# A hybrid transformer on one core: the first layer's heads in pairs, in a TensorE order written out by hand

## The chip, the cores and the metric

The kernel runs on one core of a Trainium2 chip. The metric is the device time of one execution in microseconds. It has one launch, and every input is read from HBM. In the text PE is TensorE (matmuls, transposes), DVE is VectorE, ACT is ScalarE, POOL is GpSimd and SP is SyncE, which issues most of the loads.

## What is computed

Two blocks in a row for 512 tokens of width 1024, all in fp32. The first block has a gated delta layer and a layer of stick-breaking attention; the second has sliding-window attention beside an mLSTM, and a PEER feed-forward. The change touches the gated delta layer alone. Cut to what matters:

```python
mod = silu(c) @ w_ada[layer] + b_ada[layer]          # "conditioning": shift, scale, gate
h = rms(x, norm_g) * (1 + scale) + shift
proj = h @ w_in                                      # 4096 columns: q, k, v, z of 8 heads of 128, and b, a
qkv = silu(causal_conv(proj[..., :3 * W], conv_w))   # 4 taps
q, k = l2norm(q) * Dh ** -0.5, l2norm(k)             # per head
# chunks of 64 tokens; g is the cumulated log-decay of a chunk
L = strict_lower((k_beta @ k.T) * decay)
u, w = solve(L + I, [v_beta, k_beta * exp(g)])       # triangular, 64 x 64
attn = lower((q @ k.T) * decay)
def step(S, ...):                                    # 8 chunks, one after the other
    v_new = u_i - w_i @ S
    o = q_dec_i @ S + attn_i @ v_new
    S = S * g_last_i + k_dec_i.T @ v_new
o = rms(o, o_gain) * silu(z)
x = x + gate * (o @ w_out)
```

The second layer of the block, its keys and values (`w_kv`) and the whole second block follow. Their conditioning (24 + 16 rows of 128 outputs) depends on `c` alone and is computed during the first layer.

## The kernel before

**Projections.** Activations lie transposed, width on the partitions. An fp32 product is made of three matmuls in a split format: each operand has a high and a low part (`hH`, `hL` for the activations, `wh`, `wl` for the weights), and `mm3` multiplies high by high (L106), high by low (L107) and low by high (L108). `wtile` loads a block of 128 weight columns and makes the parts two k-slices at a time: ACT the high one (L99), POOL the low one (L102), or DVE, where the running number of the weight tile (`uid`) divides by 9. One block of 128 output columns is 8 x 3 matmuls over 512 tokens. Column block `cb` is q of head `cb` for 0 to 7, k for 8 to 15, v for 16 to 23, z for 24 to 31. The result goes through `conv` (ACT, then DVE with L444 among others, tile `y`) or `silu_z`.

**One head** (`gdn_head`, L526 to L671). *Preparation*: norms of q and k from column sums, the transposes of k and v (L542 and on), decay matrices `A` and `B`, the products k·k and q·k (L576), the transposes of `B` (L589, L595), short DVE instructions on 4 columns (L546, L561) and short powers on POOL (`cols`, L549). *Inverse*: the 64 x 64 triangular matrices of all 8 chunks, two to a 128 x 128 tile, are inverted by doubling in 5 levels (L605 to L625). A level is: the masked block `Lm` on POOL (L607), the transposes of X (L611, from the second level on), 4 matmuls Y = Lm X (L616), a copy by ACT (L618), 4 matmuls (L621), and the new X by DVE (L623). Then the inverse is multiplied with `vb` and `kw` (L628 to L632). *Recurrence*: 8 chunks, each with `s<-S,WQ` (L646), u on DVE, `s<-kd,u` (L650) and the new S on DVE (L655). *Tail*: attn times u, the output's norm, transposes, and `oT`.

**Order before.** `project(0)`, then for each head `gdn_head` and the next head's `project`, in plain program order. A scheduler with a model of the engines' times then moves each engine's instructions; so projection matmuls of later heads already stand between the levels of an inverse, and heads overlap, as far as tiles have buffers and PSUM has tags (`n` with two buffers, one each of `v0`, `v1`, `s0`, `s1`, two `pj`). No line fixes PE's order.

**Conditioning.** `ada` loads 128 rows of weights (512 KB) into one of two buffers. The 48 late rows (gate of this layer, all of the next) are started by `aside`, one after each new X and each `oT`. Two are DVE reductions; 46 are a product on POOL (L176, tile `ada`), a sum on ACT (L177) and an addition on DVE (L178).

**Start and end of the layer.** Under the first norm, while the conditioning of this layer comes in, the column blocks `FIRST` = 0, 8, 16 are projected k-slice by k-slice as the norm delivers them; `A0` and `WB` are buffer counts there. At the end `residual` projects with `w_out` in two parts of k: heads 0 to 6 for all 8 blocks, then head 7 (`EARLY_A`); partial sums are added to x, the squares of the new x are added up, and PE's column sums (L114) open the next norm.

Of the kernel before, what the change touches and what calls it, by code (L numbers as in the profile page):

```python
# [10 lines left out]
F32 = mybir.dt.float32  # L11
# [8 lines left out]
P = 128  # L20
# [13 lines left out]
class Net:  # L34
# [187 lines left out]

    def wtile(self, w, j0, n=2, ks=slice(0, KC)):
# [25 lines left out]
    def proj_T(self, w, j0, nblk, act, cb, ks=slice(0, KC)):  # L249

        H, L = act
        for g in range(0, nblk, self.blocks):
# [5 lines left out]
            for j in range(n):  # L258
                p = self.pj()
                for k in range(ks.start, ks.stop):  # L260
                    wh, wl = at(k)
                    self.mm3(p, wh[:, j], wl[:, j], H[:, k], L[:, k], k == ks.start, k == ks.stop - 1)
                cb(g + j, p)
# [25 lines left out]
    def residual(self, w, act, gate, x_in, x_out, scratch=None, parts=(slice(0, KC),)):  # L289

        nc = self.nc
# [12 lines left out]
        for ks in parts:  # L304
            self.proj_T(w, 0, KC, act, lambda j, p: cb(j, p, ks is parts[0], ks is parts[-1]), ks=ks)
# [21 lines left out]
class Gdn(Net):  # L327
    SPARE_SB, SPARE_2, SPARE_P = "pj pj l l", "pj pj l l", "pj pj s s"
    RAW, SB_, PART = 3, 3, 2
    FIRST, OFF, A0, WB, SPARE_0, SQ = (0, 8, 16), (), 12, 6, "v0", 8  # L330
    SP = 5
    YB = 8
    EARLY_A, EARLY_OUT = (slice(0, 7), slice(7, 8)), (slice(0, 6), slice(6, 8))
    RATE, LV = 1.0, 100
    S1, S2, S3, R1 = (3, 4), (6, 2), (3, 4), 3

    def gdn(self):
# [5 lines left out]
        with ExitStack() as st:  # L343
            self.ring(1, self.RAW, self.SB_, self.PART)
            self.psum(st, n=2, v0=1, v1=1, s0=1, s1=1)
# [10 lines left out]
            with tc.tile_pool(name="g_t", bufs=2) as tmp, tc.tile_pool(name="g_ada0", bufs=self.A0) as ap0:  # L356
                xT = self.xtile("x0")
                self.ada_setup(ac, ap)
                for k in range(KC):
# [3 lines left out]
                    self.FIRST, (self.pj(), self.pj(), self.pg("s0"), self.pg("v0"), self.pg("v1")))}  # L363
                w16 = [tmp.tile([P, KC, 40], dt, name=f"w16{n}", bufs=1) for n, dt in (("", F32), ("h", F32R), ("l", F32R))]
                r = self.rstd(tmp, xT, "l0", psum="n")
                pba = self.pg("s1")
# [22 lines left out]
            self.spare = self.SPARE_0.split()  # L389
# [89 lines left out]
            def project(h):  # L479
                for cb in range(h, 32, 8):  # L480
                    done = (lambda j, p: conv(cb, p)) if cb < 24 else lambda j, p: silu_z(h, p)
                    if cb in first:
                        done(0, first[cb])
                    else:
                        self.proj_T(w, cb, 1, act, done)
# [5 lines left out]
            self.dump("oT", oT)  # L491
            while late or came:
                if came:
                    came.pop(0)()
                if late:
                    came.append(self.ada(ap, *late.pop(0), len(late) % self.LV != 0))
            oH = hp.tile([P, KC, T], F32R, tag="hH", name="oH")
            oL = hp.tile([P, KC, T], F32R, tag="hL", name="oL")
            for k in range(KC):
                self.split(oH[:, k], oL[:, k], oT[:, k])  # L500
            x1 = {}
# [6 lines left out]

            class Out:
# [5 lines left out]
            self.residual(a["w_out_a"], (oH, oL), self.mod0[:, 16:24], x_in, Out(), parts=self.EARLY_A)  # L515
# [10 lines left out]
    def gdn_head(self, hd, h, q, k, v, z, gcol, rows, oT):  # L526
# [3 lines left out]
        self.tag = "n"  # L530
        new = lambda tag, shape, bufs=1: hd.tile([P] + shape, F32, tag=tag, name=f"{tag}{h}", bufs=bufs)
        late = lambda tag, shape, bufs=1: self.hs.tile([P] + shape, F32, tag=tag, name=f"{tag}{h}", bufs=bufs)
        v4 = lambda t: t.rearrange("p (i c) -> p i c", i=NT)
# [16 lines left out]
        kw, kd, vb = new("kw", [NT, P], 2), late("kd", [NT, P], 2), new("vb", [NT, P], 2)  # L550
# [3 lines left out]
        kb = new("kb", [T])  # L554
        nc.vector.tensor_tensor(kb, k, self.rows_of(bk), op=ALU.mult)
        sq = new("sq", [T], 2)
        nc.scalar.activation(sq, q, AF.Square)
        p = self.pg()
        self.colsum(p, sq, 1)
        r = self.rsqrt(hd, p[:, :NT], [NT], 1.0, f"q{h}", bufs=2)  # L560
        nc.vector.tensor_scalar(rq, r, DH_SCALE, None, op0=ALU.mult)  # L561
        pG = self.rep(h, rows)
        eg = new("eg", [T])
        nc.scalar.activation(eg, pG, AF.Exp)
        A, B = late("A", [NT, P], 3), new("B", [NT, P], 2)
# [4 lines left out]
        nc.gpsimd.tensor_tensor(B, A, strm.unsqueeze(1).to_broadcast([P, NT, P]), op=ALU.mult)  # L570
        for i2 in range(0, NT, 2):
# [7 lines left out]

        WQ = late("WQ", [NT, 2, 2, 64], 2)  # L580
        c4 = lambda ap: ap.rearrange("p (i b c) -> p i b c", i=NT, b=2)
        for b in range(2):
            nc.gpsimd.tensor_tensor(WQ[:, :, b, 1 - b], c4(q)[:, :, b], c4(eg)[:, :, b], op=ALU.mult)
        gl = late("gl", [8], 2)
        nc.gpsimd.tensor_copy(gl, eg.rearrange("p (n c) -> p n c", c=64)[:, :, 63])

        p = self.pg()
        for i in range(NT):
            nc.tensor.transpose(p[:, i * P:(i + 1) * P], v[:, i * P:(i + 1) * P], self.ident)  # L589
        nc.vector.tensor_tensor(rk, rk, gcol[:, 1, :, h], op=ALU.mult)  # L590
        nc.vector.tensor_tensor(vb, v4(p), rk.unsqueeze(2).to_broadcast([P, NT, P]), op=ALU.mult)
# [6 lines left out]
        self.tag = v = f"v{h % 2}"  # L598
# [1041 lines left out]
```

## Time and profile before

| | |
|---|---|
| median of 3 runs | 2853.34 us (2845.3 to 2853.7) |
| the profiled execution | 2852.8 us, of which the trace spans 2851.0 us |
| PE busy | 2671.3 us (94%), 14601 instructions |
| DVE busy | 1786.9 us (63%) |
| ACT busy | 1210.9 us (42%) |
| POOL busy | 1765.5 us (62%) |

A matmul is pipelined and its end is modelled, so a busy PE is not PE at its peak. Busy shares are means over stages: the first layer takes the first 520 us or so of the span, and POOL is busier there than in the middle of the kernel. In rows of groups the columns are: line, engine, operation, output and inputs, shape, count | busy us, mean ns of one | idle time of the engine before them, and what ended it.

### The profile page before, as it was taken

To read this page: it belongs to the slowest core of one execution; us is meant where nothing else is said; L and a number is where in the kernel's file an instruction comes from. 1 tells how busy PE (TensorE), PEld (TensorE's weight loads), DVE (VectorE), ACT (ScalarE), POOL (GpSimd) and SP (SyncE) were. 2 spreads that over 40 slices of the span, in tenths; PEclk is the share of its full clock that TensorE was granted. 3 is DMA by queue.
4 is the path that set the end of the run, shared out by engine and by line. 5 is a ranking of instruction groups with operands and counts; after the bars stand their busy time and mean duration, and the time that the engine had idled before them with its cause. 6 is when DMAs were issued, how large, how long until landed. Compare 5 with 4: busy or idle time off the path is not lost. (4 is left out here: it accounts for less than half of the span.)

```text
span 2851.0 us, 40457 instructions
## 1 busy us (share of the span) xinstructions
PE 2671.3 (94%) x14601; PEld 2266.0 (79%) x14601; DVE 1786.9 (63%) x3095; ACT 1210.9 (42%) x2508; POOL 1765.5 (62%) x1335
## 2 busy tenths in 40 slices
PE   6999898799998999999998989998998999999999
PEld 4877777697776877778786988898998978877777
DVE  7767664614446654122332989899899166778886
ACT  5566663636654454233333333333333333333332
POOL 4889883533333522433463468788788378888786
PEclk9999999899998999999999999999999999999999
DMA  6334331221011111221222587887987879999996
GB/s 240 108 119 125 111 113 31 76 90 60 31 39 54 56 45 60 74 69 66 69 79 89 160 296 261 284 290 256 314 277 281 276 272 344 340 333 331 333 328 227
DMA packets 206793, 499.35 MB, mean 175 GB/s; under 512 B 18304, under 2 KB 106624, under 8 KB 203520
## 3 DMA queue, kind: packets, MB, share of 16 engines
q1 hardware_dynamic: 167856, 359.19, 37.6%
q0 software_dynamic: 36864, 134.23, 13.1%
q10 hardware_dynamic: 1872, 3.33, 0.4%
q8 instruction: 115, 1.88, 0.3%
q14 instruction: 86, 0.70, 0.1%
HBM read 444.26 MB, written 52.43 MB: 174 GB/s over the span
## 5 line engine op out<-in xcount | busy, mean ns | idle before, releaser
L102 POOL TENSOR_TENSOR wl<-wr,wh 128x256 fp32r<-128x256 f32 (+2 forms) x499 | 414.8, 850 | 499.2 <-ACT wh L99 468.5
L102 POOL TENSOR_TENSOR upl<-upr,uph 128x1024 fp32r<-128x1024 f32 x128 | 312.9, 2445 | 97.0 <-ACT uph L99 96.3
L99 ACT ACTIVATE wh<-wr 128x256 fp32r<-128x256 f32 (+2 forms) x556 | 228.7, 445 | 302.6 <-PE pj L107 120.4
L106 PE MATMUL pj<-nH,downh 128*128 128x384 f32 x1024 | 354.3, 346 | 2.3 <-ACT w L1459 1.7
L108 PE MATMUL pj<-nH,downl 128*128 128x384 f32 x1024 | 349.6, 341 | 4.6 <-DVE downl L102 4.6
L107 PE MATMUL pj<-nL,downh 128*128 128x384 f32 x1024 | 348.8, 341 | 0.0
L102 POOL TENSOR_TENSOR downl<-downr,downh 128x1024 fp32r<-128x1024 f32 x96 | 243.9, 2542 | 129.3 <-ACT downh L99 126.4
L1504 PE MATMUL acc<-uph,wwh 128*128 128x512 f32 x768 | 302.7, 399 | 6.9 <-ACT wwh L99 6.9
L1504 PE MATMUL acc<-upl,wwh 128*128 128x512 f32 x768 | 305.4, 398 | 0.0
L99 ACT ACTIVATE downh<-downr 128x1024 fp32r<-128x1024 f32 x128 | 135.4, 1059 | 307.0 <-PE pj L107 163.2
L102 DVE TENSOR_TENSOR wwl<-wo,wwh 128x384 fp32r<-128x384 f32 x128 | 196.1, 1533 | 76.4 <-ACT wwh L99 70.5
L1504 PE MATMUL acc<-uph,wwl 128*128 128x512 f32 x768 | 232.4, 398 | 6.6 <-DVE wwl L102 6.5
L108 PE MATMUL pj<-hH,wl 128*128 128x512 f32 x544 | 222.8, 411 | 0.9 <-POOL wl L102 0.8
L106 PE MATMUL pj<-hH,wh 128*128 128x512 f32 x544 | 220.5, 405 | 2.1 <-ACT mo L1175 1.1
L107 PE MATMUL pj<-hL,wh 128*128 128x512 f32 x544 | 215.8, 397 | 0.0
L99 ACT ACTIVATE uph<-upr 128x1024 fp32r<-128x1024 f32 x128 | 134.8, 1053 | 174.9 <-POOL upl L102 116.1
L106 PEld LDWEIGHTS pj<-nH,downh 128*128 128x128 f32 x1024 | 193.7, 189 | 6.6 <-ACT w L1459 2.0
L108 PEld LDWEIGHTS pj<-nH,downl 128*128 128x128 f32 x1024 | 193.3, 189 | 5.3 <-DVE downl L102 4.9
L107 PEld LDWEIGHTS pj<-nL,downh 128*128 128x128 f32 x1024 | 193.6, 189 | 0.0
L1428 POOL DMA_INDIRECT gdown<-in_peer_down,idx x128 | 165.7, 1295 | 44.3 <-issue 13.7
L1504 PEld LDWEIGHTS acc<-uph,wwh 128*128 128x128 f32 x768 | 145.6, 190 | 44.6 <-ACT wwh L99 9.4
L1504 PEld LDWEIGHTS acc<-uph,wwl 128*128 128x128 f32 x768 | 144.8, 189 | 43.4 <-DVE wwl L102 8.3
(621 smaller groups left out, 6702.2 us busy)
## 6 DMA issues: line engine op xcount, KB each, us to landing
downr<-in_peer_down_j SPq DMA_DIRECT2D x128, 512.0 KB, 4.8
upr<-in_peer_up_j SPq DMA_DIRECT2D x128, 512.0 KB, 6.3
wr<-in_w_in SPq DMA_DIRECT2D x50, 512.0 KB, 4.2
ada<-in_w_ada SPq DMA_DIRECT2D x48, 512.0 KB, 3.7
wait<-w SPq DMA_DIRECT2D x128, 192.0 KB, 4.9
wo<-wait SPq DMA_DIRECT2D x128, 192.0 KB, 5.2
G<-stage SPq DMA_DIRECT2D x24, 1024.0 KB, 6.9
Gt<-G SPq DMA_DIRECT2D x48, 512.0 KB, 8.0
```

The lines of the kernel that those rows point to most:

```text
L99: nc.scalar.activation(h, src, AF.Copy)
L102: return (eb or nc.vector).tensor_tensor(l, src, h.bitcast(F32), op=ALU.subtract)
L106: mm(out, lh, rh, start=start, stop=False)
L107: mm(out, lh, rl, start=False, stop=False)
L108: mm(out, ll, rh, start=False, stop=stop)
L1428: nc.gpsimd.indirect_dma_start(out=g, out_offset=None, in_=self.a[f"peer_{name}"], in_offset=bass.IndirectOffsetOnAxis(ap=self.idx[:, s:s ...
L1504: mm(po[z][b], lh[:, zs], rh[:, bs], start=False, stop=j == P - 1 and rh is uh and lh is l, skip_group_check=True)
```

## The change

The first layer is written in another order, and PE's order in it is fixed.

- `in_order` wraps the heads and the output projection: each PE instruction that is written inside must stand behind the one written before it. Only PE is ordered so; the other engines remain the scheduler's.
- `gdn_head` is cut into `gdn_prep`, `gdn_inverse`, `gdn_recur` and `gdn_tail`, generators that yield between steps; `proj_steps` and `residual_steps` yield after each k-slice (three matmuls). `weave` runs several generators in turn and gives `n` steps of a filler for each of their steps.
- Heads go in pairs. The inverses of two heads run in step, with the tails of the pair before and six projection blocks (k, q, v of the next two heads; 2 slices for a step). Then the two recurrences run in step, filled with the preparations of the next pair and their z projections (1 step for a step). The last pair is filled with the output projection (0.8 after 12 steps, then 0.5).
- `FIRST` is 0, 8, 16, 1, 9: five column blocks under the norm. `A0` 12 → 10, `WB` 6 → 10. PSUM has six buffers of one tag `n` and two of `pj`.
- `kw` is made by one DVE instruction for each head in place of four on ACT; the matmuls with `kw` come ahead of those with `vb`; the order inside the preparation is another. `kd`, `A`, `WQ` and `gl` have four buffers, `eg` and `kb` two. `EARLY_A` is heads 0 to 5, then 6 and 7.

Weight tiles get other running numbers, so other ones fall to DVE: 111 low parts in place of 57 in the whole kernel, nearly all of the difference behind this layer.

```diff
+    def in_order(self):
+        tc, bb = self.tc, self.nc.cur_bb.bb
+        n = len(bb.instructions)
+        yield
+        last = None
+        for i in list(bb.instructions)[n:]:
+            if i.engine == mybir.EngineType.PE:
+                if last is not None:
+                    tc.add_manual_dep(i, last.name, mybir.DependencyInfo(
+                        mybir.DependencyClass.NoSync, mybir.DependencyReason.DATA), reason="in_order")
+                last = i
...
-    FIRST, OFF, A0, WB, SPARE_0, SQ = (0, 8, 16), (), 12, 6, "v0", 8
+    FIRST, OFF, A0, WB = (0, 8, 16, 1, 9), (), 10, 10
-    EARLY_A, EARLY_OUT = (slice(0, 7), slice(7, 8)), (slice(0, 6), slice(6, 8))
-    RATE, LV = 1.0, 100
+    EARLY_A, EARLY_OUT = (slice(0, 6), slice(6, 8)), (slice(0, 6), slice(6, 8))
+    RATE = 1.0
+    FILL, PREP = 2.0, 1.0
...
-            self.psum(st, n=2, v0=1, v1=1, s0=1, s1=1)
+            self.psum(st, n=6)
...
-            project(0)
-            for h in range(H_):
-                self.gdn_head(hd, h, y.pop(h), y.pop(8 + h), y.pop(16 + h), y.pop(24 + h), gcol, rr, oT)
-                if h + 1 < H_:
-                    project(h + 1)
...
+            def weave(main, fill, n, skip=0):
+                main, owed, at = list(main), 0.0, 0
+                while main:
+                    for g in list(main):
+                        if next(g, self) is self:
+                            main.remove(g)
+                            continue
+                        at += 1
+                        if at > skip:
+                            owed += n
+                            run(fill, int(owed))
+                            owed -= int(owed)
...
+            with self.in_order():
+                run(project(0, 8, 16, 1, 9))
+                f = project(17, 24)
+                weave([prep(0)], f, 2)
+                run(f)
+                f = project(25)
+                weave([prep(1)], f, 1)
+                run(f)
+                tails = []
+                for h in range(0, H_, 2):
+                    last = h + 2 == H_
+                    if last:
+                        split_o(*range(h - 2))
+                        fill = self.residual_steps(a["w_out_a"], (o_["H"], o_["L"]), self.mod0[:, 16:24],
+                                                   x_in, Out(), parts=self.EARLY_A)
+                    else:
+                        fill = project(8 + h + 2, h + 2, 16 + h + 2, 8 + h + 3, h + 3, 16 + h + 3)
+                    weave([*tails, *(self.gdn_inverse(hd, h + e, heads[h + e]) for e in range(2))],
+                          fill, *((0.8, 12) if last else (self.FILL, 0)))
+                    rec = [self.gdn_recur(h + e, heads[h + e]) for e in range(2)]
+                    tails = [tail(h + e) for e in range(2)]
+                    if last:
+                        weave(rec, fill, 0.5)
...
+                    else:
+                        run(fill)
+                        fill = both(prep(h + 2), prep(h + 3), project(24 + h + 2, 24 + h + 3))
+                        weave(rec, fill, self.PREP)
+                        run(fill)
+                        for g in tails:
+                            run(g, 1)
...
-        for o, c in ((kw, kwc), (kd, gcol[:, 3, :, h])):
-            for i in range(NT):
-                nc.scalar.activation(o[:, i], pk[:, i * P:(i + 1) * P], AF.Copy, scale=c[:, i:i + 1])
+        nc.vector.tensor_tensor(kw, v4(pk), kwc.unsqueeze(2).to_broadcast([P, NT, P]), op=ALU.mult)
+        for i in range(NT):
+            nc.scalar.activation(kd[:, i], pk[:, i * P:(i + 1) * P], AF.Copy, scale=gcol[:, 3, i, h:h + 1])
```

On PE, inside an inverse, the scheduler's order before (the level's matmuls are L616 and L621, the projection's L106 to L108; numbers behind a name tell tiles apart):

```order
L616 MATMUL v049_744<-Xv00_730,Lmv00_735 128x128 x4
L108 MATMUL pj143_1935<-hH_106,wl143_1947 128x512
L106 MATMUL pj143_1935<-hH_106,wh143_1946 128x512
L107 MATMUL pj143_1935<-hL_107,wh143_1946 128x512
L108 MATMUL pj143_1935<-hH_106,wl143_1947 128x512
L106 MATMUL pj143_1935<-hH_106,wh143_1956 128x512
L107 MATMUL pj143_1935<-hL_107,wh143_1956 128x512
L616 MATMUL v180_1202<-Xv11_1194,Lmv11_1200 128x128 x4
```

And PE inside the first inverse of the changed kernel (there the transposes of X are L729, Y is L734):

```order
L729 MATMUL n81_1288<-c_id_74,Xv00_1239 128x128 x4
L734 MATMUL n82_1295<-Xv00_1239,Lmv00_1286 128x128 x4
L106 MATMUL pj84_1304<-hH_106,wh84_1305 128x512
L107 MATMUL pj84_1304<-hL_107,wh84_1305 128x512
L108 MATMUL pj84_1304<-hH_106,wl84_1306 128x512
L106 MATMUL pj84_1304<-hH_106,wh84_1305 128x512
L107 MATMUL pj84_1304<-hL_107,wh84_1305 128x512
L108 MATMUL pj84_1304<-hH_106,wl84_1306 128x512
L729 MATMUL n85_1317<-c_id_74,Xv11_1261 128x128 x4
L734 MATMUL n86_1324<-Xv11_1261,Lmv11_1315 128x128 x4
```

Before, a head's level was followed by what the scheduler found ready; now two slices of projection (six matmuls) stand between a half level of one head and that of the other, always.

On POOL, before, between the inverses (`ada` is a conditioning product, `wl` a weight split):

```order
L176 TENSOR_TENSOR ada90_1275<-ada90_1275,c_rep_118 128x1024
L102 TENSOR_TENSOR wl149_2100<-wr148_0_2086,wh149_2099 128x256
L607 TENSOR_TENSOR Lmv11_1305<-Ls1_1192,c_lv5_455 128x512
L102 TENSOR_TENSOR wl149_2110<-wr148_0_2086,wh149_2109 128x256
L176 TENSOR_TENSOR ada94_1303<-ada94_1303,c_rep_118 128x1024
L602 TENSOR_TENSOR XTv02_1709<-Ls2_1706,c_lv0_445 128x512
L607 TENSOR_TENSOR Lmv02_1714<-Ls2_1706,c_lv1_447 128x512
L102 TENSOR_TENSOR wl149_2120<-wr148_0_2086,wh149_2119 128x256
L176 TENSOR_TENSOR ada98_1331<-ada98_1331,c_rep_118 128x1024
```

And POOL in the changed kernel ahead of and in the preparation of heads 2 and 3 (beside the first recurrence):

```order
L176 TENSOR_TENSOR ada136_2083<-ada136_2083,c_rep_118 128x1024
L102 TENSOR_TENSOR wl112_1650<-wr111_0_1646,wh112_1649 128x256
L102 TENSOR_TENSOR wl116_1726<-wr111_0_1646,wh116_1725 128x256
L176 TENSOR_TENSOR ada138_2105<-ada138_2105,c_rep_118 128x1024
L102 TENSOR_TENSOR wl122_1800<-wr111_0_1646,wh122_1799 128x256
L176 TENSOR_TENSOR ada139_2133<-ada139_2133,c_rep_118 128x1024
L651 TENSOR_TENSOR cols2_1587<-kss2_1588,mhalf_72 128x4
L651 TENSOR_TENSOR cols3_1617<-kss3_1618,mhalf_72 128x4
L176 TENSOR_TENSOR ada140_2143<-ada140_2143,c_rep_118 128x1024
L176 TENSOR_TENSOR ada148_2210<-ada148_2210,c_rep_118 128x1024
```

Before, one product stands for every two to four other instructions; now they stand closer together, also between the short powers of a preparation. In the changed kernel the 46 products are spread as follows: 10 in the stretch of the first inverse and its preparation, 33 from the first recurrence to the end of the second, 3 in the third inverse, none behind it.

## Rows read from the trace of the kernel before

**Rows 1.** PE's timeline: start us, us, engine, line, form, count [wait and releaser].
```profile
524.32 1.87 PE L114 MATMUL pj<-c_one,xi 128*128 128x1 f32 x8 [5.26 <-DVE xi L198]
```
**Rows 2.** Windows: stretch, us, busy (instructions) PE, PEld, DVE, ACT, POOL, clock, DMA, GB/s.
```profile
0.00:76.00 76.00, 48.97 (x193) 34.74 (x194) 58.72 (x86) 38.92 (x72) 39.04 (x40) 1.00 0.64 231
117.00:440.00 323.00, 296.58 (x1824) 252.59 (x1822) 220.54 (x391) 199.07 (x514) 279.24 (x234) 0.97 0.35 115
...
sum 40.00, PE 36.95 PEld 30.64 DVE 32.88 ACT 27.14 POOL 39.60; mean PE 18.48 PEld 15.32 DVE 16.44 ACT 13.57 POOL 19.80
```
**Rows 3.** PE's timeline in a preparation and inverse; then one group of instructions.
```profile
166.09 0.39 PE L107 MATMUL pj<-hL,wh 128*128 128x512 f32 x1
166.32 0.38 PE L576 MATMUL n<-kb,y 128*128 128x128 f32 x2
166.54 0.39 PE L576 MATMUL n<-y,y 128*128 128x128 f32 x2
...
171.31 0.60 PE L589 MATMUL n<-c_id,y 128*128 128x128 f32 x4
171.74 1.06 PE L632 MATMUL v<-Xv,kw 128*128 128x128 f32 x8
...
L616 PE MATMUL v<-Xv,Lmv 128*128 128x128 f32 x320 | 45.3, 288 | 3.4 <-ACT XTv L613 2.7 <-POOL Lmv L607 0.6
```
**Rows 4.** PE's waits from 0 to 525 us: total us, count, longest.
```profile
PE v L611 <- DVE Xv L623: 7.9, 5, 5.6
```
**Rows 5.** POOL's groups from 60 to 525 us.
```profile
L102 POOL TENSOR_TENSOR wl<-wr,wh 128x256 fp32r<-128x256 f32 (+2 forms) x143 | 114.0, 805 | 65.9 <-ACT wh L99 61.7 <-PE pj L107 3.1 <-PE s L650 0.6
L176 POOL TENSOR_TENSOR ada<-ada,c_rep 128x1024 f32<-128x1024 f32 x46 | 110.7, 2407 | 5.6 <-DMA ada<-in_w_ada 2.9 <-DMA ada<-in_w_ada_kv 2.0 <-PE pj L108 0.3
L607 POOL TENSOR_TENSOR Lmv<-Ls,c_lv 128x512 f32<-128x512 f32 x40 | 51.5, 1288 | 13.5 <-PE v L616 13.5
L583 POOL TENSOR_TENSOR WQ<-y,eg 128x256 f32<-128x256 f32 x16 | 11.4, 734 | 1.0 <-PE s L646 0.9
L570 POOL TENSOR_TENSOR B<-A,c_str 128x512 f32<-128x512 f32 x8 | 11.3, 1409 | 0.5 <-ACT A L569 0.4
L549 POOL TENSOR_TENSOR cols<-kss,mhalf 128x4 f32<-128x4 f32 x8 | 9.4, 1169 | 1.4 <-DVE cols L548 1.1 <-ACT th L446 0.3
```
**Rows 6.** A group on DVE from 60 to 525 us.
```profile
L444 DVE SCALAR_TENSOR_TENSOR y<-pj,cwh,y 128x509 f32<-128x509 f32 (+2 forms) x69 | 50.8, 743 | 19.4 <-ACT y L442 18.5
```
**Rows 7.** PE's timeline, from the preparation of head 0 to its first level.
```profile
75.67 0.44 PE L542 MATMUL n<-c_id,y 128*128 128x128 f32 x2
...
95.22 0.60 PE L595 MATMUL n<-c_id,B 128*128 128x128 f32 x4
...
100.24 0.83 PE L616 MATMUL v<-Xv,Lmv 128*128 128x128 f32 x6
```
**Rows 8.** Groups of ACT and DVE in a level, from 60 to 525 us.
```profile
L618 ACT COPY Yv<-v 128x512 f32<-128x512 f32 x40 | 23.6, 590 | 23.4 <-PE v L616 23.0
L623 DVE TENSOR_TENSOR Xv<-Xv,v 128x512 f32<-128x512 f32 x40 | 27.3, 682 | 20.4 <-PE v L621 20.2
```
**Rows 9.** PE's timeline in the recurrence of head 7: two chunks in a row.
```profile
449.94 0.49 PE L646 MATMUL s<-S,WQ 128*128 128x128 f32 x2 [0.44 <-DVE S L655]
...
452.60 0.39 PE L646 MATMUL s<-S,WQ 128*128 128x128 f32 x2
```
**Rows 10.** Window of 100 us behind the layer, in the columns of rows 2.
```profile
1200.00:1300.00 100.00, 98.55 (x587) 79.06 (x585) 19.52 (x50) 32.58 (x96) 39.77 (x56) 1.00 0.21 69
```
**Rows 11.** Timelines of DVE, POOL and PE around 146 us.
```profile
146.28 9.93 DVE L561 TENSOR_SCALAR cols<-rv_q 128x4 f32<-128x4 f32 x1
...
135.78 2.36 POOL L176 TENSOR_TENSOR ada<-ada,c_rep 128x1024 f32<-128x1024 f32 x1
...
155.44 0.75 POOL L102 TENSOR_TENSOR wl<-wr,wh 128x256 fp32r<-128x256 f32 x1
...
157.46 1.97 PE L611 MATMUL v<-c_id,Xv 128*128 128x128 f32 x8 [5.56 <-DVE Xv L623]
```

More of the change, by code (lines that the diff above doesn't have):

```diff
@@ L1 @@
 import math
-from contextlib import ExitStack
+from contextlib import ExitStack, contextmanager
 import numpy as np
@@ L477, in gdn, with project @@
             self.aside = aside
-            def project(h):
-                for cb in range(h, 32, 8):
-                    done = (lambda j, p: conv(cb, p)) if cb < 24 else lambda j, p: silu_z(h, p)
+            def project(*cbs):
+                for cb in cbs:
+                    done = (lambda j, p, cb=cb: conv(cb, p)) if cb < 24 else lambda j, p, cb=cb: silu_z(cb - 24, p)
                     if cb in first:
@@ L484, in project @@
                     else:
-                        self.proj_T(w, cb, 1, act, done)
-            project(0)
-            for h in range(H_):
-                self.gdn_head(hd, h, y.pop(h), y.pop(8 + h), y.pop(16 + h), y.pop(24 + h), gcol, rr, oT)
-                if h + 1 < H_:
-                    project(h + 1)
[L491 to L501, printed above, removed]
+                        yield from self.proj_steps(w, cb, 1, act, done)
             def x_in(j):
@@ L507, in x_in @@
                 return t
+            x1, heads, o_ = {}, {}, {}
             class Out:
@@ L514, in __getitem__, with prep, split_o @@
                     return x1[0][at]
-            self.residual(a["w_out_a"], (oH, oL), self.mod0[:, 16:24], x_in, Out(), parts=self.EARLY_A)
+            def prep(h):
+                t = heads[h] = {}
+                return self.gdn_prep(hd, h, t, *(y.pop(n + h) for n in (0, 8, 16)), gcol, rr)
+            def split_o(*ks):
+                if not o_:
+                    o_["H"] = hp.tile([P, KC, T], F32R, tag="hH", name="oH")
+                    o_["L"] = hp.tile([P, KC, T], F32R, tag="hL", name="oL")
+                for k in ks:
+                    self.split(o_["H"][:, k], o_["L"][:, k], oT[:, k])
@@ new lines, in tail, with run @@
+            def tail(h):
+                yield from self.gdn_tail(h, heads.pop(h), y.pop(24 + h), oT)
+                if h + 4 >= H_:
+                    split_o(h)
+            def run(gen, n=10 ** 6):
+                for _ in range(n):
+                    if next(gen, self) is self:
+                        break
+            def weave(main, fill, n, skip=0):
[10 more added lines that the diff above has]
+                            owed -= int(owed)
@@ L529, in gdn_head @@
         mm = nc.tensor.matmul
[L530 to L533, printed above, removed]
+        new, late, v4 = self.gdn_tiles(hd, h)
         cols = late("cols", [4, NT], 4)
@@ L578, in gdn_head @@
                 nc.vector.tensor_tensor(x[:, i2:i2 + 2], p[:, :, a], x[:, i2:i2 + 2], op=ALU.mult)
[L580 to L591, printed above, removed]
+            yield
         p = self.pg()
@@ L668, in gdn_head @@
         nc.gpsimd.tensor_tensor(o, o, r.unsqueeze(2).to_broadcast([P, NT, P]), op=ALU.mult)
+        yield
+        for _ in range(2):
+            yield
         for i in range(NT):
```

117 lines of the change are left out of this document (93 added, 24 removed).

## The prediction

> **What bounds the kernel now.** The change touches the first layer only, so I first looked for where that layer ends: TensorE's column sums over the squares of the layer's output, which open the next norm, start at 524.3 us [rows 1]. The whole sum below is about that moment; the 2,300 us behind it are priced at its end. Next I read the busy time by stage [rows 2], to see which engine fills the layer. From 117 to 440 us, where the heads run, PE is busy 297 of 323 us and POOL 279 (86%). PE's record is not PE at its peak: a projection matmul is recorded with 0.39 us, but they start 0.23 apart; a 128-column fp32 matmul stands as two records (320 for 40 levels of 4) and takes 0.23, a transpose is one record of 0.11 [rows 3]. Counted so, from 76 us to the end the layer has 29 x 24 + 192 projection matmuls (888 x 0.23 = 204 us), and in each head 87 fp32 matmuls and 36 transposes (20 + 4 us, 192 for eight): 396 us of work in 448. PE, then, idles or runs late for 52 us, mostly in pieces that no single wait shows: the longest named one, for the inverse's new X, is 7.9 us in all [rows 4]. That is all that a better order of PE can win. Last I read POOL's groups [rows 5], since POOL is what a denser PE meets next: weight splits 114 us, products for the conditioning (tile `ada`) 111, the inverse's masked blocks 52. All of it stays; only its place moves.
>
> **The change, part by part, as a new timetable.** PE's order is fixed by hand; the others' is the scheduler's, and the built order shows it. In each part I take the engine that ends last.
>
> *Up to the first inverse.* Two more projection blocks run under the norm, where PE idles: 48 matmuls (11 us) less later. They bring 1 MB of loads into a stretch that moves 231 GB/s [rows 2]: at most 4.5 us, nothing if they fit the free third; I take 3. DVE gets four more convolution instructions ahead of head 0's preparation (20 against 16): 4 x 0.74 = 3 us [rows 6]. So it starts at 75.7 + 6 = 82. Before, it took 19.5 us from there to the transposes of B and 24.5 to the inverse [rows 7]. Head 1's stands behind it on PE, with 12 projection matmuls (2.8 us) between, and takes from 12 us (its PE work, 6.7, and 8 steps of three projection matmuls, 5.5) to the same 19.5; I take 13, as its inputs are ready by then: 82 + 19.5 + 2.8 + 13 = **117** (before: 100, with one head prepared). Bounds 113 and 124.
>
> *First inverse, two heads in step.* A level is 8 transposes, 16 fp32 and 24 projection matmuls: 0.9 + 3.7 + 5.5 = 10.1 us of PE. POOL has 2 masked blocks, 4 splits and 2 products in it: 2.6 + 3.2 + 4.8 = 10.6, and in the first none of the last. About even. Five levels (the first without transposes) and the 16 products behind them: 49.6 + 3.7 = 53 us: **170**. Bounds 51 and 58.
>
> *First recurrence, second inverse, second recurrence.* The built order shows what the sources don't: the products of the conditioning are no longer spread over all heads. 33 of the 46 stand in this stretch, ahead of and between the preparations (the POOL rows of the change). POOL's queue from here to where the third inverse begins holds 33 products, 40 splits, 12 masked blocks and 32 others (8 WQ, 12 like B, 12 short ones like `cols`): 79 + 32 + 16 + 6 + 17 + 14 = 164 us [rows 5]. PE has 31 + 62 + 31 = 124, so POOL ends last. Without a gap it is 164, at the 86% of before 190. One product is done ahead and some steps follow PE's start, which takes 4 off; I take 163, nearest to the gapless bound, since from 220 to 260 us POOL was busy 39.6 of 40 [rows 2]. **333**. Bounds 155 (each kind at its quickest) and 190.
>
> *Third inverse and recurrence.* Three products are left, so PE ends last: 62 us, less the 4.6 before the first level: 57.5 (57 to 62). The recurrence has 31 us of PE beside it, and the last pair's preparation, a chain of 24.5 us for one head [rows 7], 44 for two in a row; they run side by side and meet on DVE only: 32, as PE (31 to 44). **422**.
>
> *Last pair.* Its inverse has 36 us of PE: 25.8 of its own, 11 steps (7.6), the tails of the pair before (2.7). Two ACT copies (0.59 each) and DVE's subtraction (0.68) [rows 8] lie between a head's halves of a level, 4.6 us of PE for both heads; they fit beside the other head: 36 (35 to 40). Recurrence: a chunk of one head took 2.7 us at the best [rows 9]; two in step have 2.3 us of PE in it; 8 chunks: 21 us (18 to 29). Then 8 fp32 and 36 projection matmuls, 8 transposes, 33 and 48 more, and the last square: 1.8 + 8.3 + 0.9 + 7.6 + 11 + 2.4 = 32 us (31 to 36). 333 + 57.5 + 32 + 36 + 21 + 32 = **512**, against 524.3.
>
> kw moves from ACT (32 instructions) to DVE (8 of some 0.7 us): in the preparations, under PE or POOL. Behind the layer the built order is nearly the same, but 54 more weight splits stand on DVE in place of POOL. There PE is busy 98.6 of 100 us and DVE 20 [rows 10]; I cost it at nothing, 3 us either way.
>
> The profiled execution took 2852.8 us (span 2851.0); the runs' median is 2853.3. 2852.8 - 12.8 = **2840 us**.
>
> **Rivals.** *A held DVE* (the slower side). One DVE instruction on 4 columns was recorded with 9.93 us, from 146.3 to 156.2; POOL ran without a gap from 135.8 to 156.2, and PE stood 5.6 us for the DVE result queued behind it [rows 11]. The change makes POOL's gapless stretch longer. Each head has two such instructions (L546, L561), and one of 16 was held so long. In PE's fixed order nothing else can run meanwhile, so each hold costs up to 9.8 us: two bring the sum to 532 (no change), three decide for slower, four give 551 and 2879 us. Against it: POOL runs dry when DVE stands, which ends a hold. The Trainium skill ("GPSIMD Engine Reference", Key points) says that POOL shares its SBUF interfaces with DVE and contends with DVE instructions in a 2-port mode or with two SBUF inputs. The rows agree in that the hold ended with POOL's stretch; the time by that rule is the one just given.
>
> *POOL with gaps.* POOL must wait in the preparations for PE, ACT and DVE in turn, and for products whose two buffers are not yet loaded. At 174 us in place of 163 (94%), 36 for the third recurrence and the later parts 3 us above mine, the layer ends at 530; between 516 and 532 it is no change, 2854 us. For it: 86% is what POOL reached with the products evenly spread. Against: the gapless 40 us.
>
> *All parts at their low bounds.* 113 + 51 + 155 + 57 + 31 + 35 + 18 + 31 = 491: 2820 us. For it: PE's chains have a whole round of the other head between their halves. Against: it needs eight parts to go well.
>
> That the change does not do what it says I rule out: the built order of PE has it.
>
> **How the numbers follow.** Forecast, layer's end from 503 to 515: 0.32, 2840 us. Low bounds (below 503): 0.13, 2820. POOL with gaps: 0.27, 2854. Held DVE: 0.28, 2862 to 2890. What a measurement can tell from no change is about 0.3%, 8.6 us, so faster is 0.32 + 0.13 = 0.45, within 0.27, slower 0.28. The range goes from the low bounds to the middle of the held DVE: 2814 to 2874; the forecast's own is 2831 to 2844.
>
> **What would show it.** The column sums near 512 us; the inverse's first level at 117; POOL busy over 95% from 170 to 333 and PE short of work there; from 333 PE's starts 0.23 us apart nearly throughout. I am wrong if in the middle stretch PE is packed and POOL has gaps (then the products were no burden), if DVE records of 5 us and more stand there, or if the parts behind 333, of which only PE's work is counted, take over 190 us.

## The result and the profile after

The changed kernel is **slower**: 2899.36 us median (2895.39 to 2902.17) against 2853.52, a ratio of 1.0148 with a 95% interval of 1.0122 to 1.0173. The forecast was 2840 us, in a range from 2814 to 2874. The profiled execution took 2900.88 us, its span 2899.1 us, 48.1 more than before. One half lies in the first layer, the other behind it, where the prediction had put nothing.

TensorE's timeline of the changed kernel, cut to the starts of the stages (first level of inverses one to four, last recurrence, tail, column sums):

```profile
113.68 1.05 PE L734 MATMUL n<-Xv,Lmv 128*128 128x128 f32 x8
...
230.51 1.05 PE L734 MATMUL n<-Xv,Lmv 128*128 128x128 f32 x8
...
352.43 1.05 PE L734 MATMUL n<-Xv,Lmv 128*128 128x128 f32 x8
...
455.24 0.94 PE L734 MATMUL n<-Xv,Lmv 128*128 128x128 f32 x7
...
498.10 0.61 PE L773 MATMUL n<-S,WQ 128*128 128x128 f32 x4
...
516.38 2.05 PE L792 MATMUL n<-u,A 128*128 128x128 f32 x16 [0.31 <-ACT ot L775]
...
548.67 1.05 PE L114 MATMUL pj<-c_one,xi 128*128 128x1 f32 x8 [2.24 <-DVE xi L198]
```

The last row answers [rows 1]: 548.7 us where 524.3 stood, 24.4 later, and 36.7 later than the forecast's 512. From there to the span's end before took 2326.7 us and after 2350.4: the other 23.7.

The windows of the start and of the stretch that the prediction made POOL's (columns as in [rows 2]):

```profile
0.00:76.00 76.00, 41.23 (x164) 31.29 (x164) 54.90 (x78) 35.57 (x65) 38.27 (x38) 0.96 0.64 229
...
170.00:352.00 182.00, 149.58 (x809) 122.47 (x808) 121.16 (x204) 101.01 (x262) 157.80 (x123) 0.88 0.39 126
```

POOL is busy 157.8 of 182 us, 87%, the share that it had before [rows 2], and TensorE's granted clock is 0.88 on average. TensorE's waits from 76 us to the layer's end (total, count, longest):

```profile
PE n L446 <- DVE r_G L434: 16.6, 1, 16.6
PE n L778 <- ACT ot L775: 16.6, 12, 8.7
PE pj L108 <- POOL wl L102: 16.2, 6, 5.2
PE n L740 <- ACT Yv L736: 5.4, 3, 3.9
PE n L662 <- DVE y L473: 4.8, 1, 4.8
```

From 76 us on, the longest entry before was 7.9 us in all [rows 4]. Now three of 16 stand there: the scan of the gates ahead of the first preparation, the recurrence, and weight splits that POOL delivers late. In the fixed order TensorE can do none of the instructions behind meanwhile.

### The profile page after: what moved, and what is told of

Same layout as the page of the kernel before. It is cut to its first block, busy times and chain, and to the rows that moved or that the text cites. A ratio compares the mean times of both kernels' runs of the same rounds, so it can differ in the third digit from the quotient of the medians.

```text
span 2899.1 us, 40363 instructions
## 1 busy us (share of the span) xinstructions
PE 2680.3 (92%) x14601; PEld 2276.8 (79%) x14601; DVE 1827.2 (63%) x3157; ACT 1196.7 (41%) x2468; POOL 1731.2 (60%) x1273
## 5 line engine op out<-in xcount | busy, mean ns | idle before, releaser
L102 POOL TENSOR_TENSOR wl<-wr,wh 128x256 fp32r<-128x256 f32 (+1 forms) x429 | 364.8, 870 | 584.0 <-ACT wh L99 526.5
L99 ACT ACTIVATE wh<-wr 128x256 fp32r<-128x256 f32 (+1 forms) x540 | 223.2, 448 | 365.3 <-PE pj L107 175.6
L106 PE MATMUL pj<-nH,downh 128*128 128x384 f32 x1024 | 355.3, 347 | 5.4 <-ACT w L1596 4.5
L108 PE MATMUL pj<-nH,downl 128*128 128x384 f32 x1024 | 350.7, 343 | 0.3 <-DVE downl L102 0.3
L102 DVE TENSOR_TENSOR wwl<-wo,wwh 128x384 fp32r<-128x384 f32 x128 | 211.1, 1652 | 60.4 <-ACT wwh L99 57.3
L106 PE MATMUL pj<-hH,wh 128*128 128x512 f32 x536 | 229.7, 429 | 5.7 <-DVE nsq_q L832 2.4
L108 PE MATMUL pj<-hH,wl 128*128 128x512 f32 x536 | 217.6, 406 | 16.2 <-POOL wl L102 16.2
L106 PEld LDWEIGHTS pj<-nH,downh 128*128 128x128 f32 x1024 | 194.7, 190 | 10.0 <-ACT w L1596 5.1
L108 PEld LDWEIGHTS pj<-nH,downl 128*128 128x128 f32 x1024 | 194.4, 190 | 0.7 <-DVE downl L102 0.6
```

The costliest lines, as they stand in the source:

```text
L99: nc.scalar.activation(h, src, AF.Copy)
L102: return (eb or nc.vector).tensor_tensor(l, src, h.bitcast(F32), op=ALU.subtract)
L106: mm(out, lh, rh, start=start, stop=False)
L108: mm(out, ll, rh, start=False, stop=stop)
```

## The experiments

All times are medians; the ratio, to the kernel before on the same chip, is one of means. "Other rows" counts the rows of TensorE's built order behind the layer that differ from before (of some 10,400). "Lost in layer 2" is how much the lag against the trace of before grows between its 640th and 860th us, as the median over TensorE's instructions that both traces have. The last two columns are of the one profiled execution. The layer's end is uncertain by some 6 us by that: the changed kernel and a1 are the same program up to there and end the layer at 548.7 and 543.0, before and d2 at 524.3 and 517.5.

| kernel | fixed order | products on POOL | other rows | ratio, 95% interval | layer's end, us | lost in layer 2, us |
|---|---|---|---|---|---|---|
| before | no | 46 | 0 | 1 | 524.3 | 0 |
| changed | yes | 46 | 1494 | 1.0148 [1.0122, 1.0173] | 548.7 | 12.3 |
| a1 | yes | 46 | 107 | 1.0080 [1.0053, 1.0107] | 543.0 | 2.6 |
| a2 | yes | 46 short | 1487 | 1.0075 [1.0049, 1.0100] | 516.2 | 14.1 |
| b2 | no | 46 short | 14 | 0.9973 [0.9953, 0.9993] | 513.0 | 1.8 |
| a3 | yes | 46 | 1494 | 1.0161 [1.0125, 1.0197] | 546.0 | 14.0 |
| d1 | no | 46 | 541 | 1.0092 [1.0064, 1.0120] | 524.0 | 10.7 |
| d2 (before, renumbered) | no | 46 | 1387 | 1.0019 [0.9990, 1.0048] | 517.5 | 8.4 |
| d3 | yes | 46 | 81 | 1.0102 [1.0053, 1.0151] | 546.6 | 1.7 |
| d4 | yes | 23 | 709 | 1.0059 [1.0031, 1.0087] | 524.6 | 13.6 |
| e1 | yes | 0 | 81 | 0.9977 [0.9954, 0.9999] | 505.3 | 3.2 |
| e2 (before, 31 on DVE) | no | 15 | 105 | 1.0014 [0.9995, 1.0034] | 521.3 | 1.5 |
| e3 | yes | 31 | 14 | 1.0004 [0.9982, 1.0025] | 530.0 | 0.5 |
| e4 | no | 0 | 1177 | 1.0016 [0.9993, 1.0039] | 510.2 | 14.6 |
| f1 | no | 46 | 81 | 1.0042 [1.0027, 1.0058] | 531.9 | 0.2 |
| f2 | no | 15 | 81 | 0.9982 [0.9969, 0.9996] | 516.3 | 2.3 |
| f3 | yes | 46 | 1201 | 1.0131 [1.0107, 1.0154] | 540.7 | 10.5 |

### Behind the layer: a1 and d2

```diff
     x = net.gdn()
+    net.uid = 368        # a1, in the changed kernel; d2: 364, in the kernel before
```

> The changed kernel, with one line more: behind the first layer the running number of the tiles is set to the value that it has there in the kernel before (368 for 364), so that the same weight splits fall to DVE as before and the built order behind the layer is the old one but for some hundred of its 10,400 TensorE rows. In the changed kernel the lag against the kernel before is 24 us where the first layer ends and 48 at the end of the span. Theory A (the other 24 us come from the renumbered splits and the other order that follows from them): the lag stays near 24 us behind the layer, about 2877 us. Rival B (they come from the later start itself, or from TensorE's clock, or differ from build to build): the lag still grows by 15 us or more, 2890 us or more. In both the first layer ends at about 548 us.

Measured 2877.75 us (2876.35 to 2878.57): 21.6 less than the changed kernel (by the two ratios, some 19). Of that, 5.7 us lie in the layer, which ends at 543.0 in this execution. Theory A holds: the lag is 18.7 us at the layer's end, 21.8 from 860 to 2,000 us and 25.0 at the end of the span. Behind the layer it takes 2333.0 us, so the renumbering explains 17.4 of the 23.7 us, and 6.3 are left.

> The kernel before, with nothing changed but the running number behind the first layer: 364, as the changed kernel has it there, in place of 368. It is a1 turned round. Theory A (the number alone, through the splits that it gives to DVE and the order that follows, costs some 22 us behind the layer): 2870 to 2880 us, with the lag growing from 0 at the layer's end to some 22 at the end of the span, more than half of it between 680 and 840 us. Rival B (it costs only together with the changed first layer): within 8 us of the kernel before.

Measured 2861.85 us, a ratio that can't be told from 1, so by the median neither theory stands as written. The trace shows why it is less than 22: the same program up to the layer's end took 6.8 us less there in this execution (517.5), and behind it the lag grows by 14.8, 8.4 of that in the second layer. So the renumbering does cost behind the layer in this kernel too. TensorE's waits between 680 and 898 us show the place, first the kernel before, then the changed one, then a1:

```profile
PE l L811 <- ACT sHb_b L99: 1.2, 1, 1.2
```
```profile
PE l L948 <- ACT sHb_b L99: 10.9, 5, 6.4
```
```profile
PE l L948 <- ACT sHb_b L99: 1.2, 1, 1.2
```

It is one step of the stick-breaking attention. Where the built order is the old one it waits 1.2 us, where it is another, 8.3 (d4) to 12.8 (a2), except in d1: there it waits 2.6 us for this tile and 7.4 for another operand of the same line, `sHa_a` from DVE (2.0 before). The table's last column has no exception: the eight builds with at most 107 other rows lose 0.2 to 3.2 us there, the eight with 541 or more lose 8.4 to 14.6. It need not be the number: d1, d4, e4 and f3 have 368 as before, and the scheduler, starting from another end of the first layer, chose the other order.

### POOL's products: a2, b2, d4, e1, e2, e3

```diff
-            nc.gpsimd.tensor_tensor(raw, raw, self.c_rep, op=ALU.mult)
+            nc.gpsimd.tensor_tensor(raw[:, :4], raw[:, :4], self.c_rep[:, :4], op=ALU.mult)   # a2, b2
...
-                    came.append(self.ada(ap, *late.pop(0), True))
+                    came.append(self.ada(ap, *late.pop(0), len(late) % 2 == 0))   # d4, and net.uid = 368
+                    came.append(self.ada(ap, *late.pop(0), False))                # e1, on top of d3
+                    came.append(self.ada(ap, *late.pop(0), len(late) % 3 > 0))    # e3, on top of d3
+                    came.append(self.ada(ap, *late.pop(0), len(late) % 3 == 0))   # e2, in the kernel before
```

> The changed kernel, where each of the 46 conditioning products on POOL covers 4 of its 1024 columns (so those rows of the conditioning are wrong; loads, sums and additions stay). It takes some 106 us from POOL's queue. Theory A (the middle stretch from 170 to 352 us is POOL's queue with gaps): that stretch falls from 182 us to TensorE's own 124 plus what waits are left, 130 to 145, and the layer ends near 505; about 2855 us with the 24 us lost behind the layer. Rival B (the fixed TensorE order waits on short chains through DVE and ACT whatever POOL does, and the clock falls in each wait): the stretch stays above 165 us, 2885 us or more.

Measured 2875.23 us; the layer ends at 516.2, 32.5 earlier. The middle stretch (from the end of the first inverse's products, 176, to the third inverse, 329) is 153 us, between the two theories. So POOL's products cost this order some 30 us, yet TensorE's part alone is not 124.

> The kernel before with the same 46 products cut to 4 columns, as the control: how much POOL's products cost there. Theory A (in the kernel before TensorE is nearly packed and the products are hidden): the layer's end moves by less than 10 us, 2843 to 2853 us. Rival B (POOL bounds the kernel before as well): the end moves by 20 us or more, 2833 us or less.

Measured 2850.77 us, the end at 513.0: 11 us earlier in this trace, 7.7 us by the ratio. Theory A, within its bounds.

> As a1, but every other late conditioning row is a reduction on DVE (recorded with 1.27 us at the start of the kernel) in place of product, sum and addition on POOL, ACT and DVE: some 23 products, 55 us, leave POOL, and 29 us come to DVE. Theory A (POOL's queue, with the stands for weight splits, costs about half of what the removal of all products gave in a2, 24 us): the layer ends 8 to 16 us earlier than 543, 2862 to 2870 us. Rival B (DVE, on which TensorE's fixed order waits too, becomes the later one): no gain or a loss, 2876 us or more.

Measured 2874.24 us. In the layer theory A, and more (524.6, 18.4 earlier than a1); the second layer gave 13.6 back (a1: 2.6), where the build has the other order.

> As d3 (blocks 17 and 24 ahead, the first two preparations in step, fixed order, splits behind the layer as before), and all late conditioning rows are reductions on DVE: POOL has no product, DVE has 46 x 1.27 = 58 us more, ACT 46 sums less. The built order of the second layer is that of the kernel before. Theory A (POOL's products are what the fixed order stands behind; d4's gain of 18 us goes on): first level at 107 to 108, the layer ends at 505 to 516, nothing is lost in the second layer, 2838 to 2850 us. Rival B (DVE becomes the engine that TensorE waits for): the layer ends at 522 or later, 2855 us or more.

Measured **2846.33 us**, ratio 0.9977 [0.9954, 0.9999]: theory A, and faster than both kernels, though against the one before by 0.2% only. Whether it is the pairs that win this isn't shown: the old order with the products cut short, b2, came to 0.9973 with some of the work left out; with 31 products on DVE, e2 below, it came to 1.0014; with all 46 on DVE it wasn't run. The rows of d3 and of e1 that answer to each other, first d3 (all products on POOL), then e1:

```profile
166.00:349.00 183.00, 152.94 (x815) 124.43 (x814) 116.06 (x204) 101.19 (x262) 158.02 (x124) 0.87 0.39 126
```
```profile
165.00:312.00 147.00, 140.42 (x817) 117.07 (x816) 102.59 (x219) 70.33 (x212) 85.70 (x91) 0.95 0.27 83
```

The same 815 or so TensorE instructions take 183 us with POOL at 158 us of work, 147 with it at 86. DVE took over 48 reductions (with the two that it had) of 1.37 us, and is busy 102.6 us here, in d3 116.1. The wait for weight splits falls from 16.4 us in d3 to this in e1:

```profile
PE pj L108 <- POOL wl L102: 2.2, 3, 1.8
```

> As e1, with one in three of the rows on DVE (about 15; 31 products stay on POOL); built order of the second layer as before. Theory A (the fixed order stands in proportion to POOL's load): the layer ends between d3's 546.6 and e1's, at 528 to 540; 2860 to 2873 us, and in the second layer nothing is lost. Rival B (a step: one product less beside each level is enough): the layer ends within 5 us of e1's.

Measured 2859.50 us, the layer's end at 530.0: theory A (the median 0.5 us below its bounds). With d3 and e1, 46, 31 and 0 products on POOL give 546.6, 530.0 and 505.3, about 0.9 us for a product on average. Whether it is a line isn't shown: the medians are 2887, 2860 and 2846, 27.7 us for the first 15 products and 13.2 for the other 31, and the profiled executions of e3 and e1 lay 10 us above and 9 below their medians.

> The kernel before, with two in three of the late conditioning rows as reductions on DVE (about 31 of 46); its built order of the second layer is the old one. The control for e1: theory A (the scheduler's order had hidden the products but for the 8 us that b2 showed): the layer ends 4 to 10 us earlier, 2845 to 2852 us. Rival B (DVE's added 39 us lie on the path): no gain or a loss, 2855 us or more.

Measured 2860.98 us, no change: rival B by the time (that DVE's added work is why wasn't tested), and the layer ends only 3.0 us earlier. In the order of the kernel before, moving 31 products is worth nothing.

### The held DVE: a3

```diff
-        nc.vector.tensor_scalar(rq, r, DH_SCALE, None, op0=ALU.mult)
+        nc.scalar.activation(rq, r, AF.Copy, scale=DH_SCALE)
```

> The changed kernel with one short DVE instruction of each head (128x4, the scale of q's norm, L686, recorded with 9.38 and 3.62 us in two of 8 cases) made on ACT. Theory A (the held DVE is what costs, as the rival of the prediction has it): the stand of TensorE of 8.7 us at 204 us and the 1.2 GHz stretch behind it go, the layer ends 12 to 20 us earlier, 2880 to 2887 us. Rival B (POOL's queue sets the end of the stretch and the hold lies beside it, or another DVE instruction is held in its place): within 5 us, 2894 to 2904 us.

Measured 2900.45 us: rival B. The hold had come as the prediction feared, at 202.59 us on DVE in the changed kernel:

```profile
202.59 9.38 DVE L686 TENSOR_SCALAR cols<-rv_q 128x4 f32<-128x4 f32 x1
```

With that instruction gone, a3 has this one five microseconds later:

```profile
207.34 9.40 DVE L710 TENSOR_TENSOR Xv<-c_id,Xv 128x512 f32<-128x512 f32 x1
```

In both, the hold ends within 0.6 us of a gapless run of POOL (212.0 and 216.2 us). In the changed kernel POOL's next instruction is this:

```profile
213.49 1.28 POOL L709 TENSOR_TENSOR XTv<-Ls,c_lv 128x512 f32<-128x512 f32 x1 [1.53 <-ACT Ls L704]
```

So the hold isn't a matter of that one instruction. But a gapless run doesn't suffice for one: in a1 POOL ran for 35.5 us without a gap (190.2 to 225.8 us), and no DVE record in its layer is over 2.5 us. What starts a hold stays open. What holds cost can be estimated from two pairs of executions, each of one program up to the layer's end: a1 ends it 5.7 us before the changed kernel with its three records of 9.38, 5.90 and 3.62 us; d2, whose longest is 4.66 us, ends it 6.8 us before the kernel before with its 9.93 [rows 11]. That the holds make the whole difference isn't shown.

### The order at the start: d3

```diff
-                f = project(17, 24)
-                weave([prep(0)], f, 2)
-                run(f)
+                run(project(17, 24))
                 f = project(25)
-                weave([prep(1)], f, 1)
+                weave([prep(0), prep(1)], f, 1)
                 run(f)
```

> As a1, but the projection blocks 17 and 24 are written ahead of the first preparation, and the preparations of heads 0 and 1 then run in step with block 25 between them. In a1 TensorE stands 16.6 us (64.8 to 81.4 us) for the gates' scan on DVE, with nothing ahead of it in its order, and the clock is at 1.2 GHz from 67 to 88 us. Theory A (these 16 us are lost work): the 48 matmuls (11 us) fill the stand, the first level of the inverse starts 8 to 12 us earlier than 115.1, the layer ends 6 to 12 us earlier, 2866 to 2872 us. Rival B (DVE's convolutions and the chain through the preparation set the first level's start, whatever TensorE does): the first level starts within 4 us of 115, 2874 to 2881 us.

Measured 2887.18 us. The first level starts at 107.5, 7.6 us earlier, as theory A nearly has it, and the layer still ends at 546.6, 3.6 us later than in a1: the gain is gone at the second inverse (228 us in both). Neither theory foresaw that. In these two builds, then, when the second inverse began didn't depend on when TensorE came to the first.

### The fixed order itself: d1, e4, f1, f2

```diff
-            with self.in_order():
+            if True:
```

> As a1 (weight splits behind the layer as before), but without the fixed order: the pairs, their tiles, buffers and the written order stay, and the scheduler may move TensorE's instructions again. Theory A (what costs in the layer is that TensorE stands at an instruction of the hand order while others are ready, and that its clock falls in these stands): the layer ends 10 to 20 us earlier than in a1 (543.0), 2857 to 2867 us. Rival B (the hand order is as good as the scheduler's; POOL's queue sets the time): within 6 us of a1's 2877.8. Rival C (the hand order is what keeps it this good): 2884 us or more.

In the profile theory A (the layer ends at 524.0); by the median of 2885.31 rival C, with executions from 2867 to 2898 us and the other order in the second layer. Less the 8.1 us that d1 lost in the second layer beyond a1, the median is that of a1. That left it open, and f1 was made to settle it.

> As e1, without the fixed order on TensorE. With POOL relieved: theory A (the hand order is worth something once POOL is out of the way): the layer ends 3 us or more later than in e1. Rival B (the scheduler does as well or better): within 3 us or earlier. Its built order of the second layer is of the other kind (1,177 rows differ), so 9 to 13 us are expected to be lost between 680 and 840 us in either case.

Measured 2863.36 us; the layer ends at 510.2, 4.9 later than in e1: theory A by its bounds, but no more than two executions of one program differ by (above). By the ratios e4 is 11 us slower, and it lost 11.4 more in the second layer. That the hand order is worth something once POOL is out of the way isn't shown.

> As d3 (46 products on POOL, blocks 17 and 24 ahead), without the fixed order on TensorE; its built order of the second layer is that of the kernel before, as d3's is. It differs from d3 in the fixed order alone. Theory A (with POOL loaded the fixed order makes TensorE and POOL stand for each other; d1's profiled layer end of 524 was no accident): the layer ends 15 to 25 us before d3's 546.6, and the median is 2862 to 2872 us. Rival B (d1's median of 2885 tells the truth: the pairs cost as much in the scheduler's order): 2880 us or more.

Measured 2870.41 us, the layer's end at 531.9: theory A, 14.7 us earlier and 16.8 by the medians (d1 against a1 gives less by the times). The sources differ in the fixed order alone, the built programs don't: with it, 33 of the 46 products run in the middle stretch and 3 behind it (d3), without it 23 and 13. f1's middle stretch:

```profile
173.00:326.00 153.00, 132.39 (x773) 109.60 (x772) 112.18 (x193) 87.31 (x237) 133.41 (x115) 0.94 0.35 113
```

It is 30 us shorter than d3's, and POOL is busy 87% in it, as in the changed kernel. So f1 doesn't tell what the stands of TensorE cost and what the gathering of POOL's products does.

> As f1, with two in three of the late rows on DVE (15 products stay on POOL). Second layer's built order as before. Theory A (without the fixed order POOL's products are mostly hidden): at most 12 us faster than f1, 2852 to 2865 us, and not faster than e1 (2846). Rival B (POOL's load costs the same in any order, 0.9 us for a product): some 28 us faster than f1.

Measured 2851.00 us, 19.4 less than f1, between the theories: 0.6 us for a product, so POOL's load counts in the pairs without the fixed order too, by some two thirds of what it does with it.

### POOL's queue or the products: f3

```diff
-                    self.split(wh[:, j, o], wl[:, j, o], raw[:, fs], eb=nc.gpsimd if self.uid % 9 else nc.vector)
+                    self.split(wh[:, j, o], wl[:, j, o], raw[:, fs], eb=nc.gpsimd if self.uid % self.share else nc.vector)
# on top of d3; share is 2 in the first layer, 9 behind it
```

> As d3 (fixed order, 46 products on POOL), but about 122 more of the first layer's and the next stages' weight splits are made on DVE (every second running number in the first layer in place of every ninth): some 0.8 us each leave POOL and 0.4 us each come to DVE. Its second layer has the other built order, which costs 9 to 14 us. Theory A (POOL's queue is what costs, whatever stands in it): the layer ends 20 us or more before d3's 546.6. Rival B (it is the products themselves, through their loads, buffers or sums on ACT): the layer ends within 8 us of d3's.

Measured 2893.49 us, the layer's end at 540.7, 5.9 earlier: rival B, against me. POOL's load in the middle stretch fell from 158.0 to 137.6 us, DVE's rose from 116.1 to 152.5, and the stretch is as long as in d3. The groups on POOL and DVE say where it went, f3, from 60 us to the layer's end:

```profile
L176 POOL TENSOR_TENSOR ada<-ada,c_rep 128x1024 f32<-128x1024 f32 x46 | 112.2, 2439 | 42.3 <-DMA ada<-in_w_ada 27.6 <-DMA ada<-in_w_ada_kv 6.8 <-ACT wh L99 3.4
```
```profile
L102 DVE TENSOR_TENSOR wl<-wr,wh 128x256 fp32r<-128x256 f32 x134 | 95.3, 715 | 37.8 <-ACT wh L99 37.0
```

POOL, which runs its instructions in their order, now stood 34.4 us at products whose two buffers were not loaded again, with masked blocks queued behind them; in d3 that was 10.1 us. And a split on DVE beside the products takes 0.72 us, in e1 0.47. So the mere sum of POOL's queue doesn't set the time. A product can hold up the rest by its place in that queue, by its buffer, and by what it does to DVE; loads and ACT's sums by themselves are not the main cause, since a2 keeps both and its stretch is 153 us. How the 0.9 us for a product divides among the three, and whether DVE's greater load hid a gain here, stays open.

## Why the prediction was wrong

**The start and the first inverse** were right: first level at 113.7 (forecast 117), end of the inverse's products at 169.0 (170).

**The middle stretch** is the term that failed in the layer: 163 us forecast, 183 measured (169.0 to 352.4). Its working gave POOL 164 us of work (157.8 measured) and two ends, gapless or at 86%. I took the gapless one for a window of 40 us in which POOL had been busy 39.6 [rows 2]. That window came from an order that the scheduler made. POOL reached 87% again. The step "PE has 124, so POOL ends last" was too simple as well: with POOL relieved the stretch is 147 us in e1, since the first recurrence with its preparations lasts 52 us and not 31. So POOL had gaps, as in the kernel before, and TensorE was not packed either (the waits above, and the clock at 0.88). What shortens the stretch is fewer products in it: 147 us with none (e1), 153 with short ones (a2), 153 where the scheduler left 23 of them there (f1).

**The third pair and the last** came out at 102.8 and 93.4 us, forecast 89.5 and 89. In e1 the third takes 94.4: with POOL light, the sum of TensorE's counted work (62 and 31 us) holds there within 5 us, though its parts were 56 and 38. Of the 13 us too much in the third, 6.8 are waits for POOL's splits, though only a few products are left there; the rest was not followed up. The last pair was mis-sized whatever POOL did: in e1 it takes 99.1 us, 10 over the forecast, with 7.0 us of waits for POOL's `ot` in it.

**Behind the layer** is the other term that failed: I had "at nothing, 3 us either way", and it was 23.7. I judged the 54 moved splits by DVE's free time [rows 10] and called the order nearly the same; 1,494 rows differed, and one step of the second layer then waits 10.9 us for ACT. Of the 23.7, 12.3 lie in that layer. Ten of the kernels, the changed one among them, lose another 3 to 12 us between 860 and 1,200 us; that was not followed up.

**The rivals.** "POOL with gaps" was the right mechanism, priced at 174 in place of 183 us and with 7 us for the parts behind it (4 for the third recurrence, 3 for the rest) that took 18. "A held DVE" came true in its place, 9.38 us at 202.59 with TensorE standing for 8.67, but the execution with three of them (9.38, 5.90 and 3.62 us) ended the layer only 5.7 us after a1's, which has none, where each was priced at up to 9.8: they didn't decide. Two of the prediction's signs of being wrong stood in the trace: DVE records of 5 us and more in the middle stretch, and parts behind it that took over 190 us (196.2). The Trainium skill ("GPSIMD Engine Reference", Key points) names the shared SBUF interfaces; the runs agree in part: the longest DVE records stand beside POOL's products, and in e1 none is over 2.5 us, but in a1, with all the products, none is either. A case that joined both halves, POOL in the layer and the order behind it, was not among mine, so the range ended 25 us short.

**What was true of the idea**: with POOL relieved the pairs reach the forecast, 505.3 us in e1 where 512 stood. In part that is luck: e1 starts its first level 8 us earlier, in d3's order, its middle stretch is 16 us under the 163, its third pair 5 over and its last 10 over. And the old order came to 513.0 in b2, so that the pairs in themselves keep TensorE fuller isn't shown.

## What to carry to other kernels

An order written by hand can gather another engine's work in one stretch and take away the slack in which a scheduler hid it: moving 31 products off POOL was worth nothing in the old order and 19 us in the pairs (f2). Before writing one, look for a second engine that is nearly full (here POOL at 86%), count its work by stretch in the built order, and price it at the share that it reaches now, not at 100%. Compare the built order of everything behind a change, not only its instruction counts: here a shifted tile number, or merely another end of the stage before, chose an order that cost about 10 us in a stage that nobody touched. Judge a change on builds that agree outside it: on those, this one costs 0.8 to 1.0% (a1, d3) and not 1.5.

## What the hardware showed

A matmul on 64 rows, between others on 128, costs more than one of those. In the changed kernel's timeline the recurrence's `u,kd` (64 rows) is followed after 0.42 us, `S,WQ` (128 rows, the same 128 columns) after 0.21, and ahead of the first there is another 0.1:

```profile
198.57 0.38 PE L773 MATMUL n<-S,WQ 128*128 128x128 f32 x2
198.78 0.39 PE L695 MATMUL n<-kb,y 128*128 128x128 f32 x2
...
199.45 0.39 PE L695 MATMUL n<-y,y 128*128 128x128 f32 x2
199.77 0.48 PE L778 MATMUL n<-u,kd 64*128 64x128 f32 x2
200.19 0.49 PE L695 MATMUL n<-kb,y 128*128 128x128 f32 x2
```

A recurrence of a pair has 14 of them, some 4 us that my 31 lacked. How much of it is due to the rows and how much to the change between 64 and 128 isn't told apart here.

A stand also costs what follows it. Behind the 8.67 us TensorE's projection matmuls start 0.43 us apart, not 0.23; its granted clock is 1.2 GHz there:

```profile
212.65 0.79 PE L778 MATMUL n<-u,kd 64*128 64x128 f32 x2 [8.67 <-ACT ot L775]
213.37 0.79 PE L106 MATMUL pj<-hH,wh 128*128 128x512 f32 x1
213.96 0.63 PE L107 MATMUL pj<-hL,wh 128*128 128x512 f32 x1
214.39 0.63 PE L108 MATMUL pj<-hH,wl 128*128 128x512 f32 x1
```

From 76 us to the layer's end the clock was at that level for 65 us in the changed kernel, 32 in the one before and 34 in e1.
